# A hybrid decoder layer on one core: twelve of the 32 steps of the MLP's second product in seven products for nine, the end of the residual put first, seven weight buffers for eight

## The chip, the core and the metric

The kernel runs on one core of a Trainium2 chip. The metric is the device time of one execution in microseconds (us), lower is better. TensorE (PE) multiplies, VectorE (DVE) and ScalarE (ACT) work element by element, GpSimd (POOL) helps them, and SyncE (SP) issues the transfers from memory. Each engine runs its own list of instructions in a fixed order and stops at an instruction until what it waits for is there; everything behind that instruction waits with it.

## What is computed

One decoder layer for 256 tokens of width 2048 in float32: a norm, one input projection, a state-space group and an attention group side by side, an output projection with a residual, then a second norm and an MLP. The change touches the end of the output projection and the MLP:

```
x = x + concatenate([y_ssd, y_att], axis=-1) @ w_out
u = rmsnorm(x, g_mlp) @ w_up            # 2048 -> 8192
return x + square(relu(u)) @ w_down     # 8192 -> 2048
```

## The kernel before

**Three products for one.** A float32 operand is split into a rounded part "hi" and a rest "lo", and a product is made of hi·hi, lo·hi and hi·lo (`three`, L198, L200, L201). For each tile of weights SP loads `raw` (L150, 512 KB), ACT rounds it into the first half of a buffer `w2` (L153), and DVE subtracts to get the second half (L154). There are five `w2` buffers, and before the MLP four `raw` buffers (tag "raw"); from the MLP on four more (tag "rawm") in a pool that takes over memory of the pool `mid`, so the loads into it wait for the last users of `mid`. Weights are prepared in the order in which PE wants them, and a buffer is taken again when its last reader is done.

**Output projection and residual.** `w_out` is done in four quarters of 512 columns. After each, `residual(j)` adds the result to `xr` on DVE (L789), PE transposes it (L703), ACT scales it by the gain and rounds it (L706), and DVE makes the rest (L707); that is `x2x`, the left operand of the MLP's first product. ACT then squares the rows (L796) for the second norm. The norm's row factor is not applied to `x2x`; as `rs4` it is applied when a result is added to `xr` (L901). After the fourth quarter DVE sums the squares and makes `rs4` with 17 small instructions (L815, `rsqrt`, L817).

**The MLP in three passes.** The 32 steps of 256 hidden units are done in passes of 10, 11 and 11 (`PARTS`). In a pass `up` makes all of its steps (first product, L239, then relu and square, split into `uh` and `ul`), and `down` multiplies them with `w_down`, first for output columns 0 to 1023 (j = 0, "first half"), then for the rest ("second half"). A plain step is 8 products of 128x128x512, so 24 matmuls. For the steps of a pass whose number g is in `SEVEN` a Strassen-Winograd scheme does with 7 products, so 21 matmuls. For it `combine` makes three sums of weight blocks `t` with four POOL instructions (L861 to L864), which read and overwrite the two `raw` tiles of the step, and `combined` rounds them on ACT (L879) and takes the rest on DVE (L880) into `wt`. **There is one `t` and one `wt`.** So the wt of one such step can be rounded only after PE has done the step before it of that kind, and POOL can begin the next t only when DVE has finished this wt. In `up`, DVE makes four sums more for such a step (L838).

**The turn.** Products p1, p5, p6, p7 are summed over the steps of a half in four accumulators. After the last step of that kind, which is g = 8, DVE adds them up and empties them (L901, L934 to L940). The second half's ordinary accumulators are the same four, so PE can't begin the second half before that. Between lie g = 9 in the first pass, g = 9 and 10 in the others. The end of the first half and the start of the second is called the turn below.

**Order.** PE's instructions stand in the order in which the program issues them. For all other engines a scheduler sets the order, by place in the program and by priority: weights (`operands`, `combine`, `combined`) are raised by `HP` = 600 places. SP's loads stand in that order in one queue.

Of the kernel before, what the change touches and what calls it, by code (L numbers as in the profile page):

```python
# [1 line left out]

# [1 line left out]

# [5 lines left out]
F32 = mybir.dt.float32  # L10
# [33 lines left out]


PARTS = (0, 10, 21, 32)
SEVEN = {2, 5, 8}

A11, A21, A12, A22 = range(4)
S3, S1, S2, S4 = 1, 4, 5, 6  # L50
# [34 lines left out]
def hymba_kernel(ctx: ExitStack, tc: tile.TileContext, xn, xt, w_in, w_out, w_up, w_down, vcol, vrow, out):  # L85
# [46 lines left out]
    def raw_tile(parts, pitch):  # L132

        taken[0] += 1
        pool, tag = (mlp_pool[0], "rawm") if mlp_pool and taken[0] % 2 else (wts, "raw")
        return pool.tile([P, parts, pitch], F32, name="raw", tag=tag, bufs=RB)

    def operands(src, n, load=None, shift=0, parts=2):

# [554 lines left out]
            yield 3  # L694


    def split_rows(rows, hi, lo, k0, gain):

        for k in range(0, 4, 2):
            pt = mp("ps_sr").rearrange("p (k t) -> p k t", k=2)  # L700
            for i in range(2):
                for b in range(NB):
                    nc.tensor.transpose(pt[:, i, b * P:(b + 1) * P], rows[b][:, (k + i) * P:(k + i + 1) * P], ident)  # L703
            for i in range(2):
                kt = k0 + k + i
                nc.scalar.activation(hi[:, kt, :], pt[:, i, :], AF.Copy, scale=gain(kt))  # L706
                nc.vector.scalar_tensor_tensor(lo[:, kt, :], pt[:, i, :], gain(kt), hi[:, kt, :].bitcast(F32),  # L707
                                               op0=OP.mult, op1=OP.subtract)
            yield 0

    ys = {}

# [26 lines left out]
    def run():  # L739
        acc = in_block("k", load_x)  # L740
        spawn(head_norm(acc, [kT[:, :, b * P:(b + 1) * P] for b in range(NB)], vcp("g_k"), "k"), "k")
        acc = in_block("m0", load_n)
        spawn(stats(), "stats")
        for b in range(NB):
            evac(sm[b], acc[b][:, :96], b)
            evac(v[:, b, :208], acc[b][:, 96:M0W], b)
        spawn(index_keys(), "index_keys")
        spawn(rates(), "rates")
        for i in range(4):
            index_queries(in_pair("qi", i))  # L750
# [24 lines left out]

        def y_left(kt):
            if kt < 8:
                return yah[:, kt, :], yal[:, kt, :]
            need(f"gate{kt // 4 - 2}")
            hi, lo = ys[kt // 4 - 2]  # L780
            return hi[:, kt % 4, :], lo[:, kt % 4, :]

        ss2 = keep.tile([P, NB, 4], F32, name="ss2")
        box = []

        def residual(j, acc):
# [6 lines left out]
            yield from split_rows(rows, box[0][:, :, :T], box[0][:, :, T:], 4 * j, lambda kt: vcp("g_mlp", kt))
            for b in range(NB):
                junk = mid.tile([P, 512], F32, name="junk2", **u2)
                nc.scalar.activation(junk, rows[b], AF.Square, accum_out=ss2[:, b, j:j + 1])  # L796

        for j in range(4):
            spawn(residual(j, product(w_out[j], 512, y_left)), f"res{j}")
        return xr, box, ss2  # L800

    xr, box, ss2 = run()

    def x2(kt):
        if kt >= KT - 4:
# [6 lines left out]
    sst = keep.tile([P, NB], F32, name="sst")  # L812
    rs2 = keep.tile([P, NB], F32, name="rs2")
    rs4 = keep.tile([P, NB], F32, name="rs4")
    nc.vector.tensor_reduce(out=sst, in_=ss2, axis=AX.X, op=OP.add)  # L815
    rsqrt(rs2, sst, 1.0 / D, "x2")
    nc.vector.tensor_tensor(rs4, rs2, rs2, op=OP.mult)  # L817
    mid_stack.close()


# [3 lines left out]
    def up(h, tag):  # L824

        u = []
        for j in range(PARTS[h + 1] - PARTS[h]):
# [7 lines left out]
            if n == 7:  # L835
                for o, x, y, op in ((S1, A21, A22, OP.add), (S2, S1, A11, OP.subtract), (S3, A11, A21, OP.subtract),
                                    (S4, A12, S2, OP.subtract)):
                    nc.vector.tensor_tensor(full[:, o], full[:, x], full[:, y], op=op)  # L838
            shape = [P, 7 if j in SEVEN else 4, P]
            uh = mlp.tile(shape, F32R, name="uh", tag=f"uh{j}", bufs=1)  # L840
            ul = mlp.tile(shape, F32R, name="ul", tag=f"ul{j}", bufs=1)
            nc.scalar.copy(uh[:, :n], full[:, :n])
# [185 lines left out]
```

## Time and profile before

| | |
|---|---|
| runs | 1062.31, 1064.66, 1067.76 us; median 1064.66 |
| the profiled execution | 1066.81 us, its span from first to last instruction 1065.0 |
| TensorE clock granted in it | 0.998 |
| steps in seven products | g = 2, 5, 8 of each pass, in both halves: 18 of 64 |
| transfers | 207.41 MB, 195 GB/s over the span |

Times in rows are us from the start of the span. A matmul's duration in the rows is longer than its pitch, since matmuls overlap; where they follow each other without a gap, the pitch is the distance of two starts. In brackets stands how long the engine had been idle and what ended that.

### The profile page before, as it was taken

The page shows a single profiled execution, that of the slowest core. Times are in us where ns is not written, and L with a number is a line of the kernel's source. Part 1 is how long each engine was busy: PE and PEld are TensorE (multiplying, and loading weights), DVE is VectorE, ACT ScalarE, POOL GpSimd, SP SyncE. Part 2 cuts the span into 40 slices and gives each one's busy share as a digit, 9 for nine tenths or more (in the row PEclk, how much of TensorE's full clock was granted, in tenths as well). Part 3 has the DMA queues.
Part 4 walks back from the last instruction along what each step waited for, and adds up shares of the span by engine and source line. Part 5 has one row for each costly group of instructions (what it writes and reads, how often), then busy time and mean ns, then how long its engine had stood idle before and what let it go on. Part 6 is the DMA issues. An engine that isn't in the chain of part 4 may idle for free.

```text
span 1065.0 us, 15655 instructions
## 1 busy us (share of the span) xinstructions
PE 1057.3 (99%) x5962; PEld 936.6 (88%) x5962; DVE 785.3 (74%) x1066; ACT 555.8 (52%) x749; POOL 151.4 (14%) x102
## 2 busy tenths in 40 slices
PE   9999999999999989999999999999999999999998
PEld 7999999888888878888888889998888899988887
DVE  7776899677775656667787766768797676677885
ACT  7755464556765544454545445545544454445452
POOL 0020000122000000003352000025240000043430
PEclk9999999999999999999999999999999999999999
DMA  9865446553375565654756666547656565657561
GB/s 328 270 211 180 158 129 194 186 159 133 125 257 183 192 237 178 198 189 159 235 189 235 198 199 198 198 152 230 212 198 235 190 196 189 207 169 237 193 222 40
DMA packets 63611, 207.41 MB, mean 195 GB/s; under 512 B 7088, under 2 KB 11440, under 8 KB 63536
## 3 DMA queue, kind: packets, MB, share of 16 engines
q1 hardware_dynamic: 63392, 206.36, 58.7%
q8 instruction: 47, 0.77, 0.3%
q14 instruction: 28, 0.23, 0.1%
q10 hardware_dynamic: 144, 0.05, 0.0%
HBM read 204.29 MB, written 2.10 MB: 194 GB/s over the span
## 4 chain that ended last, share of the span: by engine, by line
PE 98%; DMA 1%; ACT 0%; DVE 0%; SPq 0%; issue 0%; ACTq 0%
PE acc L239 32%; PE acc L198 17%; PE acc L200 17%; PE acc L201 17%; PE acc L218 10%; PE ps_y L619 1%; DMA raw<-in_w_up 1%; PE ps_l L657 0%; PE ps_o L682 0%; PE ps_sr L703 0%; DMA xT<-in_xt 0%; PE ps_s L510 0%; PE ps_s L509 0%; PE ps_dec L610 0%; PE ps_pt L674 0%; DVE w L154 0%
## 5 line engine op out<-in xcount | busy, mean ns | idle before, releaser
L154 DVE TENSOR_TENSOR w<-raw,w 128x1024 fp32r<-128x1024 f32 (+3 forms) x364 | 439.4, 1218 | 197.0 <-ACT w L153 195.2
L153 ACT CAST w<-raw 128x1024 fp32r<-128x1024 f32 (+3 forms) x364 | 359.6, 993 | 330.4 <-PE acc L201 139.3
L239 PE MATMUL acc<-x2x,w 128*128 128x512 f32 (+2 forms) x2053 | 347.6, 330 | 2.7 <-DVE x2x L707 2.7
L239 PEld LDWEIGHTS acc<-x2x,w 128*128 128x128 f32 x2053 | 309.9, 188 | 39.7 <-DVE x2x L707 3.5
L198 PE MATMUL acc<-w,uh 128*128 128x512 f32 (+5 forms) x459 | 168.6, 373 | 0.0
L200 PE MATMUL acc<-w,ul 128*128 128x512 f32 (+1 forms) x444 | 168.1, 379 | 0.0
L201 PE MATMUL acc<-w,uh 128*128 128x512 f32 (+1 forms) x444 | 168.1, 379 | 0.0
L861 POOL TENSOR_TENSOR t<-raw 128x512 f32<-128x512 f32 x18 | 25.9, 1440 | 645.4 <-DMA raw<-in_w_down 482.7
L218 PE MATMUL acc<-hx,w 128*128 128x256 f32 (+1 forms) x978 | 115.0, 277 | 0.0
L218 PEld LDWEIGHTS acc<-hx,w 128*128 128x128 f32 x978 | 112.7, 188 | 0.0
L198 PEld LDWEIGHTS acc<-w,uh 128*128 128x128 f32 x459 | 85.9, 188 | 14.6
L200 PEld LDWEIGHTS acc<-w,ul 128*128 128x128 f32 x444 | 83.4, 188 | 13.7
L201 PEld LDWEIGHTS acc<-w,uh 128*128 128x128 f32 x444 | 83.3, 188 | 13.6
L198 PE MATMUL acc<-w,hx 128*128 128x512 f32 (+3 forms) x228 | 84.0, 371 | 0.3 <-ACT hx L277 0.3
L200 PE MATMUL acc<-w,hx 128*128 128x512 f32 (+1 forms) x224 | 81.0, 361 | 0.0
L201 PE MATMUL acc<-w,hx 128*128 128x512 f32 (+1 forms) x224 | 80.8, 361 | 0.0
L880 DVE TENSOR_TENSOR w<-raw,w 128x1024 fp32r<-128x1024 f32 x36 | 56.4, 1566 | 20.5 <-ACT w L879 18.4
L879 ACT CAST w<-raw 128x1024 fp32r<-128x1024 f32 x36 | 37.7, 1046 | 41.9 <-PE acc L201 36.8
L880 DVE TENSOR_TENSOR wt<-t,wt 128x1536 fp32r<-128x1536 f32 x18 | 31.6, 1757 | 25.9 <-ACT wt L879 25.9
L198 PEld LDWEIGHTS acc<-w,hx 128*128 128x128 f32 x228 | 42.8, 188 | 6.7 <-issue 0.7
L200 PEld LDWEIGHTS acc<-w,hx 128*128 128x128 f32 x224 | 42.2, 188 | 6.0 <-issue 0.7
L201 PEld LDWEIGHTS acc<-w,hx 128*128 128x128 f32 x224 | 42.1, 188 | 6.0 <-DVE w L154 0.4
(229 smaller groups left out, 1043.8 us busy)
## 6 DMA issues: line engine op xcount, KB each, us to landing
raw<-in_w_up SPq DMA_DIRECT2D x128, 512.0 KB, 4.3
raw<-in_w_down SPq DMA_DIRECT2D x128, 512.0 KB, 4.3
raw<-in_w_in SPq DMA_DIRECT2D x72, 512.0 KB, 3.9
raw<-in_w_out SPq DMA_DIRECT2D x32, 512.0 KB, 3.3
raw<-in_w_in SPq DMA_DIRECT2D x16, 256.0 KB, 5.4
raw<-in_w_in SPq DMA_DIRECT2D x16, 152.0 KB, 5.1
raw<-in_w_in SPq DMA_DIRECT2D x8, 304.0 KB, 3.2
xT<-in_xt SPq DMA_DIRECT2D x8, 256.0 KB, 5.4
```

What stands on the lines that cost most here:

```text
L153: nc.scalar.copy(hi[:, s], raw[:, s, :n])
L154: nc.vector.tensor_tensor(lo[:, s], raw[:, s, :n], hi[:, s].bitcast(F32), op=OP.subtract)
L198: nc.tensor.matmul(go(out[:, i:j]), ah, go(wh[:, i:j]), start=first and i == 0, stop=False, skip_group_check=True)
L200: nc.tensor.matmul(go(out), al, go(wh), start=False, stop=False, skip_group_check=True)
L201: nc.tensor.matmul(go(out), ah, go(wl), start=False, stop=last, skip_group_check=True)
L218: nc.tensor.matmul(acc[:, c, at:at + n], w[:, 0, s], x[:, fr:fr + n], start=(i + k + j == 0), stop=(i >= 2 and k == 7 and j == len(todo) - ...
L239: nc.tensor.matmul(walk(out[:, at:at + n]), w[:, 0, s], walk(x[:, at:at + n]), start=(i < 2 and k + j == 0), stop=(i >= 2 and k == 7 and j ...
L619: nc.tensor.matmul(pt[:, 64 * i:64 * i + 64], m[i // 4][:, i % 4, :], xdt[:, c, 64 * h:64 * h + 64], start=True, stop=True)
L861: nc.gpsimd.tensor_tensor(t[:, 0], raws[1][:, 1], raws[1][:, 0], op=OP.subtract)
L879: nc.scalar.copy(hi, raw)
L880: nc.vector.tensor_tensor(lo, raw, hi.bitcast(F32), op=OP.subtract)
```

## The change

1. `SEVEN` is {2, 4, 6, 8} instead of {2, 5, 8}: 24 of 64 half-steps in seven products. POOL's, ACT's and DVE's work for `t`, `wt` and the four sums is done for six more.
2. From the MLP on there are seven `raw` buffers, four of tag "raw" and three of tag "rawm", taken in turn, instead of eight.
3. The fourth quarter's additions, rounding and rests have a priority above that of weights (`urgent`), and its two groups of transposes stand together.
4. Its squares and the row factors are taken in the first `up`, at step 3 (`row_factors`), and write to tiles of the MLP's pool, not of `mid`.

```
-SEVEN = {2, 5, 8}
+SEVEN = {2, 4, 6, 8}
...
-        pool, tag = (mlp_pool[0], "rawm") if mlp_pool and taken[0] % 2 else (wts, "raw")
-        return pool.tile([P, parts, pitch], F32, name="raw", tag=tag, bufs=RB)
+        pool, tag, n = (mlp_pool[0], "rawm", 3) if mlp_pool and taken[0] % 7 in (1, 3, 5) else (wts, "raw", RB)
+        return pool.tile([P, parts, pitch], F32, name="raw", tag=tag, bufs=n)
...
+            with urgent():
+                for i in range(2):
+                    kt = k0 + k + i
+                    nc.scalar.activation(hi[:, kt, :], pt[:, i, :], AF.Copy, scale=gain(kt))
...
+            if urgent is nullcontext or k == 2:
+                yield 0
...
+            urgent = (lambda: tc.high_priority(offset=3 * HP)) if j == 3 else nullcontext
+            with urgent():
+                for b in range(NB):
+                    nc.vector.tensor_tensor(rows[b], rows[b], acc[b], op=OP.add)
+        def squares(j, rows, junk):
+            for b in range(NB):
+                nc.scalar.activation(junk[b], rows[b], AF.Square, accum_out=ss2[:, b, j:j + 1])
...
+    def row_factors(junk):
+
+        squares(3, [xr[:, b, 1536:] for b in range(NB)], junk)
+        nc.vector.tensor_reduce(out=sst, in_=ss2, axis=AX.X, op=OP.add)
+        rsqrt(rs2, sst, 1.0 / D, "x2")
+        nc.vector.tensor_tensor(rs4, rs2, rs2, op=OP.mult)
...
+            if h == 0 and j == 3:
+                row_factors([mlp.tile([P, 7, P], F32, name="r")[:, :4].rearrange("p k t -> p (k t)") for _ in range(NB)])
```

Lines move by 16 in the MLP: L879 and L880 become L895 and L896, L901 becomes L917, L934 to L939 become L950 to L955, and L706, L707 become L707, L708.

**ACT at the end of the output projection.** `ps_sr` are the transposes of the fourth quarter, `w2` the weights that follow, `junk2` the squares. Before:

```order
L796 ACTIVATE junk2_4065,ss2_3350<-xr_3345 128x512
L796 ACTIVATE junk2_4067,ss2_3350<-xr_3345 128x512
L706 ACTIVATE x2x_3547<-ps_sr_4024,vc_86 128x256 x2
L153 CAST w2_4151<-raw_4150 128x1024
L153 CAST w2_4172<-raw_4171 128x1024
L153 CAST w2_4193<-raw_4192 128x1024
L706 ACTIVATE x2x_3547<-ps_sr_4047,vc_86 128x256 x2
```

And now:

```order
L707 ACTIVATE x2x_3547<-ps_sr_4024,vc_86 128x256
L707 ACTIVATE x2x_3547<-ps_sr_4033,vc_86 128x256
L707 ACTIVATE x2x_3547<-ps_sr_4024,vc_86 128x256
L153 CAST w2_4148<-raw_4147 128x1024
L707 ACTIVATE x2x_3547<-ps_sr_4033,vc_86 128x256
```

The squares are gone from here, and one cast of weights stands ahead of the last of the four roundings, where three stood ahead of the last two.

**SP in the second pass, ahead of the turn.** The first two rows are weights of the second half's g = 0, the next two (L859, now L875) are those of its g = 2, which POOL combines. The brackets name whose count each load waits for. Before:

```order
L150 DMA raw_7274<-in_w_down 128x1024 [waits DMAHW6_49,DMAHW4_49,DVE_49]
L150 DMA raw_7279<-in_w_down 128x1024 [waits DMAHW7_49,DMAHW5_49,DVE_49]
L859 DMA raw_7308<-in_w_down 128x1024 [waits DVE_49,Pool_49]
L859 DMA raw_7310<-in_w_down 128x1024 [waits DVE_49]
L150 DMA raw_7317<-in_w_down 128x1024 [waits DMAHW0_49,DVE_49]
```

And now:

```order
L150 DMA raw_7296<-in_w_down 128x1024 [waits DMAHW7_49,DMAHW4_49,DVE_49]
L150 DMA raw_7301<-in_w_down 128x1024 [waits DMAHW5_49,DVE_49,Pool_49]
L875 DMA raw_7330<-in_w_down 128x1024 [waits DVE_49]
L875 DMA raw_7332<-in_w_down 128x1024 [waits DMAHW2_49,DVE_49]
L150 DMA raw_7339<-in_w_down 128x1024 [waits DMAHW0_49,DVE_49]
```

The wait for POOL has moved up by one load; what `raw_7301` takes over is the first `raw` tile of g = 8, which POOL reads last in its fourth instruction. In the first pass the same wait stood at the load behind the two of g = 2 and now stands at the second of the two.

**DVE in the second pass, at the turn.** `wt_7357` and now `wt_7379` belong to the second half's g = 2; `r` are sums of the accumulators; `w2_7280`, `w2_7323` and now `w2_7302`, `w2_7345` are weights of the second half's g = 0 and g = 1. Before:

```order
L934 TENSOR_TENSOR r_7187<-r_7187,acc_6949 128x512
L935 TENSOR_TENSOR r_7188<-r_7187,acc_6950 128x512
L880 TENSOR_TENSOR wt_7357<-t_7312,wt_7357 128x1536
L901 SCALAR_TENSOR_TENSOR xr_3345<-r_7188,rs4_4113,xr_3345 128x512
L937 TENSOR_TENSOR r_7187<-r_7187,acc_6948 128x512
L939 TENSOR_TENSOR r_7188<-r_7188,acc_6948 128x512
L154 TENSOR_TENSOR w2_7280<-raw_7279,w2_7280 128x1024
```

And now:

```order
L950 TENSOR_TENSOR r_7209<-r_7209,acc_6966 128x512
L951 TENSOR_TENSOR r_7210<-r_7209,acc_6967 128x512
L896 TENSOR_TENSOR wt_7379<-t_7334,wt_7379 128x1536
L917 SCALAR_TENSOR_TENSOR xr_3345<-r_7210,rs4_4108,xr_3345 128x512
L953 TENSOR_TENSOR r_7209<-r_7209,acc_6965 128x512
L955 TENSOR_TENSOR r_7210<-r_7210,acc_6965 128x512
L154 TENSOR_TENSOR w2_7302<-raw_7301,w2_7302 128x1024
```

Nothing moved here: as before, the next half's wt stands between the first and the last of the sums, ahead of weights that PE needs sooner. In the first pass it stands in the same place.

## Rows read from the trace of the kernel before

**Rows 1.** The page's first part: busy us, share of the span, instructions.

```profile
PE 1057.3 (99%) x5962; PEld 936.6 (88%) x5962; DVE 785.3 (74%) x1066; ACT 555.8 (52%) x749; POOL 151.4 (14%) x102
```

**Rows 2.** Who waited for whom, of PE: us in total, times, longest.

```profile
PE acc L239 <- DVE x2x L707: 2.7, 2, 2.4
```

**Rows 3.** The timeline of all engines from the last matmuls of the output projection into the MLP's first product.

```profile
384.52 0.63 ACT L796 ACTIVATE junk<-xr 128x512 f32<-128x512 f32 x1 [1.89 <-DVE xr L789]
...
390.01 2.00 ACT L153 CAST w<-raw 128x1024 fp32r<-128x1024 f32 x2 [0.49 <-DMA raw<-in_w_up]
...
392.54 1.04 ACT L153 CAST w<-raw 128x1024 fp32r<-128x1024 f32 x1 [0.52 <-DMA raw<-in_w_up]
393.49 0.47 ACT L706 ACTIVATE x2x<-ps_sr,vc 128x256 fp32r<-128x256 f32 x1
...
395.27 0.47 ACT L706 ACTIVATE x2x<-ps_sr,vc 128x256 fp32r<-128x256 f32 x1 [1.31 <-DVE x2x L707]
395.29 0.30 PEld L239 LDWEIGHTS acc<-x2x,w 128*128 128x128 f32 x2 [2.74 <-DVE x2x L707]
395.29 0.79 PE L239 MATMUL acc<-x2x,w 128*128 128x512 f32 x2 [2.44 <-DVE x2x L707]
...
396.31 3.80 PEld L239 LDWEIGHTS acc<-x2x,w 128*128 128x128 f32 x15 [0.73 <-DVE x2x L707]
```

**Rows 4.** The timeline of PE in the second product: in the first pass the first matmul of g = 8 of the first half, of g = 9, and the first matmul of the second half that writes p5's accumulator; in the second pass the first matmul of g = 8, and the matmuls that first read the lo of `w2_7280` and of `w2_7323`.

```profile
540.53 0.38 PE L198 MATMUL acc<-w,uh 128*128 128x512 f32 x1
...
545.15 0.38 PE L198 MATMUL acc<-w,uh 128*128 128x512 f32 x1
...
551.75 0.38 PE L198 MATMUL acc<-w,uh 128*128 128x512 f32 x1
...
759.94 0.38 PE L198 MATMUL acc<-w,uh 128*128 128x512 f32 x1
...
776.88 0.38 PE L201 MATMUL acc<-w,uh 128*128 128x512 f32 x1
...
782.16 0.38 PE L201 MATMUL acc<-w,uh 128*128 128x512 f32 x1
```

**Rows 5.** Groups of instructions by line and shape: count, busy us, mean ns of one, idle time before them.

```profile
L880 DVE TENSOR_TENSOR wt<-t,wt 128x1536 fp32r<-128x1536 f32 x18 | 31.6, 1757 | 25.9 <-ACT wt L879 25.9
...
L838 DVE TENSOR_TENSOR r<-r 128x128 f32<-128x128 f32 x36 | 11.8, 349 | 0.6
...
L879 ACT CAST wt<-t 128x1536 fp32r<-128x1536 f32 x18 | 26.5, 1474 | 39.8 <-POOL t L864 27.0 <-PE acc L201 12.8
```

**Rows 6.** Line L880's instructions on the two `raw` tiles: shortest, median and longest duration in ns.

```profile
L880 DVE TENSOR_TENSOR w<-raw,w x36: 1208/1226/2309, 503.1 to 1040.7; 128x1024 fp32r<-128x1024 f32 x36
```

**Rows 7.** The timeline of POOL: the start of the combination for the second half's g = 2 in the first pass; then the first and the last instruction of that combination in the second pass; then of one in its second half.

```profile
534.76 1.29 POOL L861 TENSOR_TENSOR t<-raw 128x512 f32<-128x512 f32 x1 [8.77 <-DMA raw<-in_w_down]
...
759.51 1.28 POOL L861 TENSOR_TENSOR t<-raw 128x512 f32<-128x512 f32 x1 [14.61 <-DMA raw<-in_w_down]
...
765.35 2.15 POOL L864 TENSOR_TENSOR t<-raw,t 128x512 f32<-128x512 f32 x1
...
793.89 1.28 POOL L861 TENSOR_TENSOR t<-raw 128x512 f32<-128x512 f32 x1 [7.86 <-DVE wt L880]
...
798.85 2.15 POOL L864 TENSOR_TENSOR t<-raw,t 128x512 f32<-128x512 f32 x1
```

**Rows 8.** The timeline of DVE in the first pass: the wt of g = 5, then, at the turn, the wt of the second half's g = 2 and the first and the last of the sums behind it.

```profile
516.55 1.76 DVE L880 TENSOR_TENSOR wt<-t,wt 128x1536 fp32r<-128x1536 f32 x1 [0.15 <-ACT wt L879]
...
548.12 1.75 DVE L880 TENSOR_TENSOR wt<-t,wt 128x1536 fp32r<-128x1536 f32 x1
549.78 0.74 DVE L901 SCALAR_TENSOR_TENSOR xr<-r,rs,xr 128x512 f32<-128x512 f32 x1
...
551.04 0.68 DVE L939 TENSOR_TENSOR r<-r,acc 128x512 f32<-128x512 f32 x1
```

**Rows 9.** The timeline of ACT: the wt of g = 5 in the first pass, and the wt of the second half's g = 2 in the second pass.

```profile
515.04 1.48 ACT L879 CAST wt<-t 128x1536 fp32r<-128x1536 f32 x1 [0.99 <-PE acc L201]
...
767.53 1.47 ACT L879 CAST wt<-t 128x1536 fp32r<-128x1536 f32 x1 [3.71 <-POOL t L864]
```

**Rows 10.** The timeline of DVE at the turn of the second pass: the wt of the second half's g = 2, then `w2_7280` and `w2_7318`, then `w2_7323`.

```profile
769.82 1.75 DVE L880 TENSOR_TENSOR wt<-t,wt 128x1536 fp32r<-128x1536 f32 x1
...
773.34 2.35 DVE L154 TENSOR_TENSOR w<-raw,w 128x1024 fp32r<-128x1024 f32 x2
...
778.91 1.50 DVE L154 TENSOR_TENSOR w<-raw,w 128x1024 fp32r<-128x1024 f32 x1
```

**Rows 11.** The timeline of SP: the two loads for the combination that begins at 534.76.

```profile
528.25 1.47 SPq L859 DMA_DIRECT2D raw<-in_w_down  x2
```

**Rows 12.** The page's sixth part: issues, KB each, median us from issue to landing.

```profile
raw<-in_w_down SPq DMA_DIRECT2D x128, 512.0 KB, 4.3
```

**Rows 13.** Busy us of each engine and instructions in two stretches, with clock, DMA share and GB/s: one in the first `up`, one in the first half of the first pass.

```profile
432.00:443.00 11.00, 11.00 (x66) 9.73 (x65) 6.86 (x8) 5.30 (x9) 0.00 (x0) 1.00 0.64 195
500.00:530.00 30.00, 30.00 (x141) 25.71 (x140) 25.50 (x21) 17.22 (x19) 13.88 (x8) 1.00 0.67 225
```

More of the change, by code (lines that the diff above doesn't have):

```diff
@@ L1 @@
-from contextlib import ExitStack
+from contextlib import ExitStack, nullcontext
 import numpy as np
@@ L694, in attention, with split_rows @@
             yield 3
-    def split_rows(rows, hi, lo, k0, gain):
+    def split_rows(rows, hi, lo, k0, gain, urgent=nullcontext):
         for k in range(0, 4, 2):
@@ L703, in split_rows @@
                     nc.tensor.transpose(pt[:, i, b * P:(b + 1) * P], rows[b][:, (k + i) * P:(k + i + 1) * P], ident)
[L704 to L709, printed above, removed]
+            with urgent():
+                for i in range(2):
+                    kt = k0 + k + i
+                    nc.scalar.activation(hi[:, kt, :], pt[:, i, :], AF.Copy, scale=gain(kt))
+                    nc.vector.scalar_tensor_tensor(lo[:, kt, :], pt[:, i, :], gain(kt), hi[:, kt, :].bitcast(F32),
+                                                   op0=OP.mult, op1=OP.subtract)
+            if urgent is nullcontext or k == 2:
+                yield 0
     ys = {}
@@ L784, in run @@
         box = []
+        def squares(j, rows, junk):
+            for b in range(NB):
+                nc.scalar.activation(junk[b], rows[b], AF.Square, accum_out=ss2[:, b, j:j + 1])
         def residual(j, acc):
             rows = [xr[:, b, 512 * j:512 * j + 512] for b in range(NB)]
-            for b in range(NB):
-                nc.vector.tensor_tensor(rows[b], rows[b], acc[b], op=OP.add)
+            urgent = (lambda: tc.high_priority(offset=3 * HP)) if j == 3 else nullcontext
+            with urgent():
+                for b in range(NB):
+                    nc.vector.tensor_tensor(rows[b], rows[b], acc[b], op=OP.add)
             yield Y["res"] if j < 3 else 1
@@ L792, in residual @@
                 box.append(keep.tile([P, KT, 2 * T], F32R, name="x2x", tag="hx"))
[L793 to L796, printed above, removed]
+            yield from split_rows(rows, box[0][:, :, :T], box[0][:, :, T:], 4 * j, lambda kt: vcp("g_mlp", kt),
+                                  urgent)
+            if j < 3:
+                squares(j, rows, [mid.tile([P, 512], F32, name="junk2", **u2) for _ in range(NB)])
         for j in range(4):
             spawn(residual(j, product(w_out[j], 512, y_left)), f"res{j}")
-        return xr, box, ss2
-    xr, box, ss2 = run()
+        return xr, box, ss2, squares
+    xr, box, ss2, squares = run()
     def x2(kt):
@@ L814, in hymba_kernel @@
     rs4 = keep.tile([P, NB], F32, name="rs4")
-    nc.vector.tensor_reduce(out=sst, in_=ss2, axis=AX.X, op=OP.add)
-    rsqrt(rs2, sst, 1.0 / D, "x2")
-    nc.vector.tensor_tensor(rs4, rs2, rs2, op=OP.mult)
+    def row_factors(junk):
[3 more added lines that the diff above has]
+        nc.vector.tensor_tensor(rs4, rs2, rs2, op=OP.mult)
     mid_stack.close()
```

## Prediction

> **What bounds the kernel now.** First the busy shares: PE is busy for 1057.3 of 1065.0 us, so only fewer matmuls, or a wait of PE that goes or comes, can move the end [rows 1]. Then PE's waits: but for the first microseconds they name one place, 2.7 us where the first product of the MLP needs `x2x` [rows 2]. Then the timeline there: three casts of later weights stand ahead of the last two roundings, and the third waits for a load; ACT rounds at 393.49 and 395.27 what PE wanted 2.44 us before 395.29 [rows 3]. Last the second product, where PE never waits; the question is by how much the others are ahead of it. DVE is busy for 25.50 of 30 us there [rows 13], and the turn shows the margin: the last sum that empties p5's accumulator ends at 551.04 + 0.68 = 551.72, and PE's first matmul into it starts at 551.75 [rows 4, 8]. **There is no slack at the turn of the first pass.**
>
> **Fewer matmuls.** 21 of them take 545.15 - 540.53 = 4.62 us, so 0.220 each, and a plain step of 24 takes 5.28 [rows 4]. Three steps more in two halves save three matmuls each: 18 x 0.220 = **4.0 us**, all on the path.
>
> **The end of the residual.** PE's idle time of 2.44 us and the small one behind it make the 2.7 us [rows 2, 3]. Three of the four roundings now stand ahead of any cast, with the transposes together. The last stands behind one cast, whose load no longer waits for the squares, that is until 384.52 and over a microsecond of ACT. If the load starts with the end of the output projection, at about 384.2, and takes the median 4.3 us [rows 12] or, several together, some two more, then a cast, a rounding and a rest (1.04 + 0.47 + 0.5) make it ready by 390.5 to 392.5; PE wants it just past 395.29 - 2.44 = 392.85. So the stall goes: **2.7 us**. Ends: 0.5 less where the load is late, and 3.5 by the weight loads' idle times (2.74 + 0.73) [rows 3].
>
> **Costs that I put at nothing.** The 17 small instructions and two squares move into an `up` where DVE is idle for 4 of 11 us and ACT for more than 5 [rows 13], with five `w2` buffers between them and PE; uncovered they would cost some 3 us once. The four sums for one step more per pass (4 x 0.35 us [rows 5]) lie in the same slack. Seven loads under way for eight matter nothing in `up`, where a tile lasts PE longer than the 4.3 us that it takes to land.
>
> **The loop of t and wt.** This is the cost that decides. With steps of that kind two apart, PE has 21 + 24 = 45 matmuls, 9.9 us, for one round of the loop. The round: POOL's four instructions, 759.51 to 767.50, so 8.0 us, or 793.89 to 801.00, so 7.1 [rows 7]; ACT's wt 1.47; DVE's wt 1.76 [rows 5]; three handovers of 0.03 to 0.08. That is **10.5 to 11.4 us**: longer than PE's 9.9. (Three apart, PE needed 15.2, and the loop had time to wait.) I take 8.0 for POOL: its long instructions of 2.15 us fall beside DVE's, and DVE has more to do now.
>
> Let S be the start of g = 8 in the first half. PE ends g = 2 114 matmuls before it, at S - 25.1. ACT starts the wt of the next such step 0.25 us after that (515.04, where by the matmuls g = 2 ends at 540.53 - 117 x 0.22 = 514.79), and DVE ends it at 518.31 [rows 8, 9]: S - 21.6. Two rounds later the wt of g = 8 is ready, at S - 0.6 to S + 1.2. PE wants it at S + 2.6, after four products, so it is in time by 1.4 us at worst. But the loop arrives late at the turn, and there the next half's wt stands in DVE's list ahead of what PE needs.
>
> **First pass.** POOL is through with g = 8 3.3 us before its wt, at S - 3.9 to S - 2.1. With seven buffers the second load for the next combination waits for that; it lands 4.3 us later (3.3 to 5.4; the two loads issued from 528.25 on were waited for until 534.76 [rows 7, 11, 12]). POOL runs from then, or from when t is free, takes 7.1 to 8.0, and rounding and rest take 3.3: wt at S + 9.9 to S + 14.6. Before: 549.87 - 540.53 = S + 9.3 [rows 4, 8]. At POOL's 8.0 and 4.3 for the load it is S + 13.5, 4.2 later. The next combination then starts beside the sums, and the first of these (0.67 us in its place) reads two operands from SBUF as L880 does, which goes from 1226 to 2309 ns beside POOL [rows 6]: 0.6 more. With no margin, PE waits **4.8 us** (0.6 to 5.9).
>
> **Second and third pass, each.** One plain step more lies in between, but now the wait for POOL stands one load ahead of both loads for the combination, so three are issued at POOL's end. At 225 GB/s with a share of 0.67 [rows 13] 512 KB take 1.6 us at full rate: the last lands after 4.4 to 7.5, and I take 6.0. POOL starts at S + 3.9 and wt is there at S + 15.2 (10.9 to 16.7), against 771.57 - 759.94 = S + 11.6 before: 3.6 later. Two weights behind it run beside POOL, 1.1 us longer each [rows 6], and one that was slowed by 0.3 is no longer. `w2_7323` had ended at 780.4 for a matmul at 782.16 [rows 4, 10], a margin of 1.75: 3.6 + 2.2 - 0.3 - 1.75 = **3.75 us** (0 to 5.5). The wait comes in two pieces, at g = 0 and g = 1 of the second half. Second halves have no turn of this kind behind them: nothing.
>
> Sum: + 4.8 + 2 x 3.75 - 4.0 - 2.7 = **+ 5.6 us** on the span of 1065.0, so 1070.6; the runs' median stands 0.3 below this span (and the profiled execution 1.8 above), so **1070.3**. Ends of the terms: + 0.6 - 4.0 - 3.5 = - 6.9, and 5.9 + 11.0 - 4.0 - 2.2 = + 10.7.
>
> What POOL and DVE do to each other is shown by rows: 1.28 for 2.15 us and 1226 for 2309 ns [rows 6, 7]. The Trainium skill, page "SBUF — State Buffer", section "Who interferes with whom", says that a DVE instruction with two SBUF inputs contends with a reading GpSimd, and that the loser fully blocks for the whole instruction. The long POOL instruction agrees only roughly: 2.15 us is less than 1.28 + 1.21. Taken strictly it gives the fourth rival.
>
> **Rivals.**
> 1. *The cover holds*, the one that ends faster. Price: nothing at the turns, - 6.7, so 1058. It decides at POOL's 7.1 us: then the loop slips only 0.6 a round, and quick loads leave the turn where it was. For it: PE never waited here before. Against: the margin of 0.03 us, and that ACT already waited 3.71 us for POOL at the second turn with steps three apart [rows 9].
> 2. *Only the first turn stalls*: the extra plain step hides the others. 4.8 - 6.7: 1063.
> 3. *The residual keeps its stall* because the load ahead of the last rounding is late as before: 2.7 more than forecast, 1073. Against: what it waited for has gone.
> 4. *POOL blocks for a whole DVE instruction*: 1.28 + 1.21 = 2.5 for 2.15, a combination of 10.2 for 8.0 us; three in a row up to the turn are 6.6 more in three passes: 20 us, 1090. For it: 2309 ns is near 1226 + 1280. Against: 2.15 was the longest usual row.
>
> **How the numbers follow.** About 0.5% is what a measurement of this kernel can tell from no change: below 1059.3 is faster, above 1070.0 slower. The forecast, stalls of 9 to 17 us in all, has 58%, of which 36 above 1070.0 and 22 below. Rival 1 has 13% (12 faster, 1 the same), rival 2 15% (the same), rival 3 6% and rival 4 8% (slower). Faster 12%, the same 22 + 1 + 15 = 38%, slower 36 + 6 + 8 = 50%. The range 1060 to 1077 leaves out most of rival 1 and of rival 4. The sign is less sure than the mechanism: the forecast lies on the edge of what can be told.
>
> **What would show it.** Right: PE's matmuls fall by 18 x 128x512; no wait for `x2x`; PE waits at the first turn for L955, by 3 to 6 us, and at the other two for L154 by 2 to 6 each, in two pieces; ACT's wait for POOL grows from 27.0 us, and POOL's rounds in a half are over 10.5 us apart. Wrong: no wait of PE at the turns (rival 1), waits at wt itself (rival 4), or a wait for `x2x` still there (rival 3).

## The result: slower, by twice the forecast

The changed kernel takes 1075.80 us (median of 1073.67, 1075.61, 1075.99 and 1077.47), the kernel before 1064.83 in the same runs: ratio 1.0104, 95% interval 1.0083 to 1.0124, so **+11.0 us** where + 5.6 was forecast. The profiled execution took 1073.67, with a span of 1071.9 against 1065.0.

**Where PE waits.** The view of waits, PE alone: us in total, times, longest.

```profile
PE acc L201 <- DVE w L154: 6.9, 4, 3.1
PE acc L198 <- DVE r L955: 3.8, 1, 3.8
```

The wait for `x2x` [rows 2] is gone; instead PE waits once for p5's accumulator (the first turn) and in two pieces each at the other two turns (the four times of L154): 10.7 us in all, where 12.3 was forecast. So waits grew by 8.0 and 4.0 us of matmuls went, which would make + 4.0. The rest is not in this view.

**The turns.** The timelines of ACT, DVE and POOL. ACT's rows are the wt of g = 6, of g = 8 and of the second half's g = 2 in the first pass, then the wt of the second half's g = 2 in the second pass. DVE's rows are the same two wt of a second half and what stands behind them; POOL's row is the start of the combination for the second of them.

```profile
519.93 1.47 ACT L895 CAST wt<-t 128x1536 fp32r<-128x1536 f32 x1 [2.47 <-POOL t L880]
...
531.34 1.48 ACT L895 CAST wt<-t 128x1536 fp32r<-128x1536 f32 x1 [1.61 <-POOL t L880]
...
543.61 1.47 ACT L895 CAST wt<-t 128x1536 fp32r<-128x1536 f32 x1 [6.09 <-POOL t L880]
...
768.27 1.47 ACT L895 CAST wt<-t 128x1536 fp32r<-128x1536 f32 x1 [7.46 <-POOL t L880]
```

```profile
545.11 1.76 DVE L896 TENSOR_TENSOR wt<-t,wt 128x1536 fp32r<-128x1536 f32 x1 [1.38 <-ACT wt L895]
...
548.05 0.68 DVE L955 TENSOR_TENSOR r<-r,acc 128x512 f32<-128x512 f32 x1
...
769.77 1.76 DVE L896 TENSOR_TENSOR wt<-t,wt 128x1536 fp32r<-128x1536 f32 x1 [5.46 <-ACT wt L895]
...
773.30 3.44 DVE L154 TENSOR_TENSOR w<-raw,w 128x1024 fp32r<-128x1024 f32 x2
```

```profile
761.96 2.19 POOL L877 TENSOR_TENSOR t<-raw 128x512 f32<-128x512 f32 x1 [7.47 <-DVE w L154]
```

The round of the loop is 531.34 - 519.93 = 11.4 us, then 12.3 across the turn. ACT waits for POOL, DVE for ACT, and PE for what stands behind the wt in DVE's list: 548.05 + 0.68 = 548.73, and PE starts at 548.79. Before, DVE came to the same wt without waiting [rows 8, 10].

The matmul that waits is the tenth of the second half: the first starts at 542.80, and the first row here is the ninth. The second row is the tenth in the kernel before:

```profile
544.56 0.39 PE L201 MATMUL acc<-w,uh 128*128 128x512 f32 x1
```

```profile
552.41 0.38 PE L198 MATMUL acc<-w,uh 128*128 128x512 f32 x1
```

The last sum had ended at 551.72 [rows 8], so the kernel before had a margin of 0.69 us here.

**What a wait left behind.** PE's timeline in the first pass, behind its wait of 3.84 us, and 48 us later; then in the second pass, behind the longest wait.

```profile
548.79 0.50 PE L198 MATMUL acc<-w,uh 128*128 128x512 f32 x1 [3.84 <-DVE r L955]
549.12 0.39 PE L200 MATMUL acc<-w,ul 128*128 128x512 f32 x1
...
596.62 0.39 PE L201 MATMUL acc<-w,uh 128*128 128x512 f32 x1
596.85 0.39 PE L198 MATMUL acc<-w,uh 128*128 128x512 f32 x1
597.08 0.38 PE L200 MATMUL acc<-w,ul 128*128 128x512 f32 x1
597.30 0.39 PE L201 MATMUL acc<-w,uh 128*128 128x512 f32 x1
...
783.30 0.79 PE L201 MATMUL acc<-w,uh 128*128 128x512 f32 x1 [3.09 <-DVE w L154]
783.89 0.63 PE L198 MATMUL acc<-w,uh 128*128 128x512 f32 x1
784.32 0.63 PE L200 MATMUL acc<-w,ul 128*128 128x512 f32 x1
...
789.36 0.38 PE L200 MATMUL acc<-w,ul 128*128 128x512 f32 x1
789.58 0.38 PE L201 MATMUL acc<-w,uh 128*128 128x512 f32 x1
```

Stretches around that last wait: length, busy PE, matmuls in brackets, granted clock, DMA share and GB/s:

```profile
775.00:780.00 5.00, 5.00 (x24) 1.00 0.61 210
780.00:785.00 5.00, 1.91 (x5) 0.74 0.13 35
785.00:790.00 5.00, 5.00 (x14) 0.57 0.98 304
790.00:795.00 5.00, 5.00 (x24) 1.00 0.83 272
```

Two things follow a wait. **The clock:** behind the wait at 783 the clock is at its lower level, 1.2 GHz (0.43 between starts for 0.22, until 789.0): thirteen matmuls in 5.7 us for 2.9. **The pitch:** in the first pass the clock is 1.00, and yet starts are 0.23, 0.23, 0.22 apart instead of 0.220 [rows 4], and stay so to the end of the half: 597.30 - 549.12 is 48.18, or 211 matmuls at 0.2283, 1.8 us more than at 0.220. No idle time is shown, and PE counts as busy. The first product has it too. PE busy in L239 alone, the first `up` of the kernel before, then that of the changed one (columns as above):

```profile
380.00:500.00 120.00, 112.37 (x643) 0.99 0.59 194
```

```profile
380.00:500.00 120.00, 107.37 (x642) 1.00 0.62 202
```

The same matmuls took 5.0 us more behind the wait for `x2x`, beside its 2.7 us of idle time; the clock is part of it, as a view of the kernel before shows (0.66 for 5 us, 1.7 us lost):

```profile
395.00:400.00 5.00, 4.47 (x16) 0.66 0.65 214
```

Stage by stage, from the starts of the stages' first matmuls in the two timelines:

| stage | before | after | difference |
|---|---|---|---|
| up to the first `up` | 384.02 | 384.49 | + 0.5 |
| first `up` | 115.28 | 107.84 | - 7.4 |
| first `down` | 101.95 | 106.58 | + 4.6 |
| second `up` | 117.46 | 117.44 | 0.0 |
| second `down` | 112.51 | 119.03 | + 6.5 |
| third `up` | 117.45 | 117.45 | 0.0 |
| third `down`, to the last matmul | 112.86 | 115.56 | + 2.7 |

That is the + 6.9 of the two spans. The + 0.5 lies ahead of the MLP; that stretch takes 382.9 to 385.2 us in the runs below. The profiled execution of the changed kernel was the quickest of its four (granted clock 0.997; the others 0.995, 0.994 and 0.994), and that of the kernel before was one of its slower ones.

### The profile page after: what moved, and what is told of

Same layout as the page of the kernel before. It is cut to its first block, busy times and chain, and to the rows that moved or that the text cites. A ratio compares the mean times of both kernels' runs of the same rounds, so it can differ in the third digit from the quotient of the medians.

```text
span 1071.9 us, 15705 instructions
## 1 busy us (share of the span) xinstructions
PE 1055.4 (98%) x5943; PEld 932.2 (87%) x5943; DVE 818.1 (76%) x1084; ACT 562.3 (52%) x755; POOL 201.7 (19%) x126
## 4 chain that ended last, share of the span: by engine, by line
PE 75%; POOL 9%; issue 6%; DVE 4%; DMA 4%; ACT 1%; SPq 0%; POOLq 0%; DVEq 0%
PE acc L239 26%; PE acc L201 12%; PE acc L198 11%; PE acc L200 11%; PE acc L218 10%; DMA raw<-in_w_down 4%; POOL raw L878 3%; DVE w L154 2%; POOL t L879 2%; POOL t L877 2%; POOL t L880 2%; DVE xr L917 1%; ACT wt L895 1%; PE ps_y L619 1%; DMA xT<-in_xt 1%
## 5 line engine op out<-in xcount | busy, mean ns | idle before, releaser
L154 DVE TENSOR_TENSOR w<-raw,w 128x1024 fp32r<-128x1024 f32 (+3 forms) x352 | 428.2, 1225 | 175.0 <-ACT w L153 174.6
L153 ACT CAST w<-raw 128x1024 fp32r<-128x1024 f32 (+3 forms) x352 | 346.2, 991 | 302.3 <-PE acc L201 115.7
L239 PE MATMUL acc<-x2x,w 128*128 128x256 f32 (+2 forms) x2052 | 342.6, 327 | 0.0
L239 PEld LDWEIGHTS acc<-x2x,w 128*128 128x128 f32 x2052 | 307.9, 188 | 34.2
L198 PE MATMUL acc<-w,uh 128*128 128x512 f32 (+4 forms) x435 | 161.5, 377 | 3.8 <-DVE r L955 3.8
L877 POOL TENSOR_TENSOR t<-raw 128x512 f32<-128x512 f32 x24 | 39.3, 1636 | 613.7 <-DMA raw<-in_w_down 277.0
L896 DVE TENSOR_TENSOR w<-raw,w 128x1024 fp32r<-128x1024 f32 x48 | 87.4, 1833 | 6.0 <-ACT w L895 5.5
L895 ACT CAST w<-raw 128x1024 fp32r<-128x1024 f32 x48 | 50.3, 1048 | 37.6 <-PE acc L201 19.1
L895 ACT CAST wt<-t 128x1536 fp32r<-128x1536 f32 x24 | 35.4, 1474 | 65.3 <-POOL t L880 62.8
L896 DVE TENSOR_TENSOR wt<-t,wt 128x1536 fp32r<-128x1536 f32 x24 | 42.2, 1757 | 33.4 <-ACT wt L895 33.1
L198 PEld LDWEIGHTS acc<-w,hx 128*128 128x128 f32 x228 | 42.7, 188 | 7.5 <-ACT w L153 1.1
L878 POOL TENSOR_TENSOR raw<-raw 128x512 f32<-128x512 f32 x24 | 47.5, 1977 | 1.9
```

Of the source, the lines that this page charges most:

```text
L153: nc.scalar.copy(hi[:, s], raw[:, s, :n])
L154: nc.vector.tensor_tensor(lo[:, s], raw[:, s, :n], hi[:, s].bitcast(F32), op=OP.subtract)
L198: nc.tensor.matmul(go(out[:, i:j]), ah, go(wh[:, i:j]), start=first and i == 0, stop=False, skip_group_check=True)
L239: nc.tensor.matmul(walk(out[:, at:at + n]), w[:, 0, s], walk(x[:, at:at + n]), start=(i < 2 and k + j == 0), stop=(i >= 2 and k == 7 and j ...
L877: nc.gpsimd.tensor_tensor(t[:, 0], raws[1][:, 1], raws[1][:, 0], op=OP.subtract)
L878: nc.gpsimd.tensor_tensor(raws[1][:, 0], raws[1][:, 0], raws[0][:, 0], op=OP.subtract)
```

## The experiments

Theory A: a wait of PE costs its length and, behind it, a lower clock for some us and a wider pitch. B: a wait costs its length alone. C: the seven buffers make the turns wait. D: the loop of t and wt is too slow at distance two, whatever stands where at the turn. Each table line gives the medians of the kernel and of the kernel before on the same chip.

| run | us | before | difference | ratio, 95% interval |
|---|---|---|---|---|
| e1_three | 1061.22 | 1063.63 | - 2.4 | 0.9970 to 0.9986 |
| e1b_three_eight | 1059.77 | 1063.63 | - 3.9 | 0.9956 to 0.9980 |
| e2_seven_only | 1076.62 | 1063.63 | + 13.0 | 1.0109 to 1.0154 |
| e3_hold | 1061.28 | 1063.63 | - 2.4 | 0.9970 to 1.0003 |
| e4_wait | 1067.75 | 1063.98 | + 3.8 | 1.0014 to 1.0044 |
| e5_wait_cuts | 1064.06 | 1063.98 | + 0.1 | 0.9996 to 1.0015 |
| e6_short_wait | 1059.57 | 1063.98 | - 4.4 | 0.9948 to 0.9975 |
| e7_best | 1058.08 | 1063.98 | - 5.9 | 0.9935 to 0.9969 |
| e8_twenty_two | 1059.61 | 1064.01 | - 4.4 | 0.9947 to 0.9974 |
| e9_after_cuts | 1075.25 | 1064.01 | + 11.2 | 1.0081 to 1.0126 |
| e10_urgent | 1060.06 | 1064.01 | - 4.0 | 0.9951 to 0.9975 |
| e11_wait_again | 1068.21 | 1064.01 | + 4.2 | 1.0025 to 1.0057 |
| e13_hold_first_22 | 1058.23 | 1064.14 | - 5.9 | 0.9931 to 0.9960 |
| e14_pool_three | 1056.44 | 1064.14 | - 7.7 | 0.9912 to 0.9938 |
| e15_after_again | 1076.23 | 1064.14 | + 12.1 | 1.0080 to 1.0145 |

**The parts of the change.** e1_three is the changed kernel with

```
-SEVEN = {2, 4, 6, 8}
+SEVEN = {2, 5, 8}
```

> The changed kernel with SEVEN back at {2, 5, 8}: the new residual, the late row factors and seven raw buffers alone. A (a wait of PE costs its length, and behind it a lower granted clock for some us and a wider pitch of matmuls to the end of the stage): no wait for x2x, no low clock behind it, first up 107.8 us as in the changed kernel and not 115.3; 1064.8 - 7.4 = 1057.4, and no wait at a turn. B (a wait costs its length and no more): 1064.8 - 2.7 = 1062.1. C (seven buffers are what makes the turns wait): waits of 1 to 3 us at the turns here too, 1060 to 1066.

e1b_three_eight has the eight buffers of before as well:

> The same with eight raw buffers as before: the residual and the late row factors alone. A: 1057.4, within 1 us of the run with seven. B: 1062.1. C: 3 to 6 us less than with seven.

e2_seven_only is the kernel before with `SEVEN = {2, 4, 6, 8}` and the seven buffers:

> The kernel before with SEVEN {2, 4, 6, 8} and seven raw buffers, its residual as it was: four seven-product steps a half alone. A: the wait for x2x and its 7.4 us stay, so 1075.8 + 7.4 = 1083. B: 1075.8 + 2.7 = 1078.5. In both PE waits at the turns for 3 to 4 us each, in the first pass for L939 and in the others for L154.

e10_urgent is the kernel before with the `urgent` lines alone:

> The kernel before with the priority of the residual's last quarter alone: squares and row factors stay where they were, SEVEN {2, 5, 8}, eight buffers. All four roundings now stand ahead of the casts of the first weights, and the squares ahead of both. If the order on ACT was what made PE wait for x2x: the wait goes, 1059.8 as with the late row factors. If the late load was it (it waits for the squares): PE waits 1 to 3 us for the first weights of up instead, 1061 to 1064.

e10 and e1b give the same - 4.0 and - 3.9: the priority alone is enough, and the late squares and row factors add nothing that can be measured. PE waits nowhere in the MLP in either, and their first `up` is busy for 107.37 as in the changed kernel. The median gain lies between B (2.7) and A's 7.4; A's figure came from a dear execution. Of the 23 executions of the kernel before beside e1b those with a clock of 0.998 took 1062.8 to 1066.7 and those with 1.0 took 1061.8 to 1063.3; beside e10, on another chip, some with 1.0 took up to 1066.6, so the clock is not all of it.

Seven buffers for eight cost 1.4 us in the medians (e1 against e1b), but the two intervals overlap. In the profiles the difference is 1.3 us, all of it in the second half of the first pass, where e1's starts are 0.2233 apart and e1b's 0.220; an execution with eight buffers shows the same pitch there (e5, below). So C is not shown. With {2, 4, 6, 8} eight buffers were not run; e3 and e13 below keep the seven and lose the waits for L154.

e2 carries the whole loss, with waits of 2.9 and 7.1 us at the same lines as the changed kernel (its L939 is L955 there). A's 1083 was missed (B's 1078.5 lies inside the interval), and what both took for granted doesn't hold: its profile has no wait for `x2x` either. ACT there, in the numbers of the kernel before:

```profile
390.73 1.05 ACT L153 CAST w<-raw 128x1024 fp32r<-128x1024 f32 x1
391.69 0.47 ACT L706 ACTIVATE x2x<-ps_sr,vc 128x256 fp32r<-128x256 f32 x1
```

One cast stands ahead of the last rounding, as in the changed kernel, and PE is busy in its first `up` for 107.77. So e2's own edits, the buffers or the four steps, change the order on ACT without the priority, and beside them the priority adds nothing that can be measured (1076.62 against 1075.80). If its other executions lack that wait too, the turns cost e2 13.0 + 4.0 for the matmuls + 4.0 for the residual = 21 us.

**The order at the turn.** e3_hold makes the second half's wt wait for the weights that PE needs sooner:

```
 w = combined(ahead, w[1][1][1][:, :1] if j == 1 and g == min(marked) else None) if seven ...
...
+    if n == 3 and hold is not None:
+        nc.vector.tensor_copy(hi[:, 0, :1], hold)
     nc.scalar.copy(hi, raw)
```

> The changed kernel, but the wt of the second half's g = 2 waits for the second half's g = 1: a copy of one column from its last w2 into wt ahead of ACT's rounding. Everything else as in the changed kernel. A: no wait at a turn, and with the waits their clock and pitch go too: 1064.8 - 7.4 - 4.0 = 1053.4. B: 1075.8 - 10.7 = 1065.1. D (the loop of t and wt itself is too slow for steps two apart, whatever its place in the order at the turn): waits for wt of 1 to 4 us in a half, 1058 to 1070.

One instruction of 0.14 us in each second half (L896, a copy of one column) takes 13.4 us off the changed kernel (+ 11.0 to - 2.4). PE's waits:

```profile
PE acc L201 <- DVE wt L898: 2.1, 2, 1.1
...
PE acc L198 <- DVE r L957: 0.9, 1, 0.9
```

Waits fell by 7.7 us and the time by 13.4: B is refuted. The 1053.4 was missed, though, and D explains part: in the first pass, where the sums still came 0.9 late, wt is twice late by 1.07. ACT's wt there:

```profile
565.12 1.48 ACT L897 CAST wt<-t 128x1536 fp32r<-128x1536 f32 x1 [1.60 <-POOL t L880]
...
576.51 1.47 ACT L897 CAST wt<-t 128x1536 fp32r<-128x1536 f32 x1 [1.60 <-POOL t L880]
...
587.92 1.47 ACT L897 CAST wt<-t 128x1536 fp32r<-128x1536 f32 x1 [1.61 <-POOL t L880]
```

Rounds of 11.4 us, and PE takes 9.9 for one. e14_pool_three leaves out one of POOL's four instructions in it, L878's `raws[1][:, 0] - raws[0][:, 0]`, so that it computes no layer:

> As e3_hold (1061.3, two waits of 1.07 us for wt in the first pass, rounds of 11.4 us), with POOL's second instruction of four left out, which takes the difference of two blocks in place; the products of the steps concerned are then not the layer's. D: rounds of 9.3 to 10 us, no wait for wt, 1056 to 1059. If POOL's share of the round isn't what sets it (DVE's and ACT's order is): rounds stay near 11, waits for wt stay.

```profile
562.62 1.47 ACT L896 CAST wt<-t 128x1536 fp32r<-128x1536 f32 x1 [4.80 <-POOL t L879]
...
572.65 1.48 ACT L896 CAST wt<-t 128x1536 fp32r<-128x1536 f32 x1 [3.64 <-POOL t L879]
...
582.69 1.48 ACT L896 CAST wt<-t 128x1536 fp32r<-128x1536 f32 x1 [4.78 <-POOL t L879]
```

Rounds of 10.0, no wait for wt, 1056.4: POOL's share sets the round, and the loop is D's, but it is worth some 5 us at the most, not the 20 or so of the turns.

e14 also gives a price by stage, since its profile has the changed kernel's 5943 matmuls and no wait in the MLP. By the starts of the stages its three `down` are 1.32 us shorter each than e1b's: the 4.0 us of the 18 matmuls. Those of the changed kernel are 5.9, 7.8 and 4.0 us longer than e14's, **17.8 us for 10.7 of waiting**; e2's are 19.9 longer for 10.3.

**The price of a wait by itself.** e4_wait puts a wait into e1b, where there was none; e6_short_wait has the same with `(3, 0)` and `range(2)`:

```
+if h > 0 and j == 1 and g == 1:
+    spare = [mlp.tile([P, 7, P], F32, name="r").rearrange(...) for _ in range(2)]
+    with tc.high_priority(offset=3 * HP):
+        for i in range(4):
+            nc.scalar.copy(spare[i // 2][:, 448 * (i % 2):448 * (i % 2) + 448], outs[(3, 2, 1, 0)[i]][:, :448])
```

> The kernel with the new residual, SEVEN {2, 5, 8} and eight buffers (1059.8), in which PE waited nowhere in the MLP, with one wait put in at the start of g = 1 of the second half, in the second and third pass: ACT copies 448 columns of each of the four open accumulators to unused memory, and PE's next matmul into the last of them waits for that. Two waits of 2.5 to 3.3 us. A (a wait of PE costs its length, and behind it a lower granted clock for some us and a wider pitch of matmuls to the end of the half): 2 x 3 for the waits, 0 to 3.4 each for the clock, 0.8 to 1.8 each for the pitch of the 220 matmuls behind: 1068 to 1074, clock 0.995 to 0.998. B (a wait costs its length): 1066, clock 1.0.

> The same without splits, with two copies instead of four: two waits of 1.2 to 2.2 us. A: the pitch widens as behind the longer wait, the clock falls more rarely: 2 x 1.7 + 2 x 1.3 + 0 to 2 = 1065 to 1068. B: 1063.

> The same kernel as e4_wait, for a second profile: e4_wait's profiled execution was its fastest (1061.9, pitch 0.220 throughout), its median 1067.8 at a clock of 1.0. If the wider pitch is what the slower ones pay, a profile of a usual one shows two waits of 1.5 us as before, clock 1.0, and a pitch of 0.223 to 0.229 from one or both waits to the end of the half, or a longer third up.

In e6 no wait came about, against the expectation: both copies ran under matmuls that don't need them, and its 1059.57 is e1b's 1059.77. So the two copies cost nothing, and e4's two waits of 1.54 us (shorter than expected) cost 1067.75 - 1059.57 = **8.2 us for 3.1 of waiting, at a clock of 0.999 to 1.0**: neither B nor the clock, but the pitch. The first profile was of an execution without it, the second, e11, with. PE behind the first of the two waits, in e4 and then in e11:

```profile
773.56 0.49 PE L198 MATMUL acc<-w,uh 128*128 128x512 f32 x1 [1.54 <-ACT r L964]
773.89 0.39 PE L200 MATMUL acc<-w,ul 128*128 128x512 f32 x1
774.12 0.38 PE L201 MATMUL acc<-w,uh 128*128 128x512 f32 x1
774.34 0.38 PE L198 MATMUL acc<-w,uh 128*128 128x512 f32 x1
...
822.30 0.38 PE L201 MATMUL acc<-w,uh 128*128 128x512 f32 x1
```

```profile
775.49 0.50 PE L198 MATMUL acc<-w,uh 128*128 128x512 f32 x1 [1.54 <-ACT r L964]
...
777.17 0.38 PE L200 MATMUL acc<-w,ul 128*128 128x512 f32 x1
...
825.86 0.38 PE L198 MATMUL acc<-w,uh 128*128 128x512 f32 x1
```

The wait is the same to the hundredth. In e4 the 219 matmuls from 774.12 to 822.30 are 0.220 apart; in e11 the 218 from 777.17 to 825.86 are 0.2233 apart. And e11's third `up`, which begins behind such a half, is busy for 120.73 us where e4's takes 117.61 (L239, the first row e4, the second e11):

```profile
820.00:960.00 140.00, 117.61 (x705) 1.00 0.61 194
```

```profile
820.00:960.00 140.00, 120.73 (x705) 1.00 0.58 188
```

So the wider pitch takes 0.7 us in each half, and something like it outlives the stage: 3.1 us in the `up` between them. In all, from the first `up` on, e4's profile is 3.7 us longer than e1b's, and e11's 8.3, for the same 3.1 us of waits.

e5_wait_cuts adds to e4 split matmuls behind the waits, such as `CUTS` makes where a first half begins:

```
+if h > 0 and j == 1:
+    cut = {8 + at: n for at, n in CUTS.items()}
```

> The same with five matmuls of the steps behind the wait split in two, as the kernel does it at the start of each first half (CUTS). A: the waits as in the run without splits, the pitch back at 0.220 within 6 us of the wait, so 1 to 3 us less; the clock falls as there. If the pitch has nothing to do with the wait, no change or up to 1 us more for the splits.

It took 3.7 us off e4, with the same two waits of 1.54 in its profile, where the pitch is 0.220 again from 785 on; but e4's own profile is back at 0.220 without splits, so only the medians speak for them.

The profile of e5 is of its slowest execution, 1066.83, and shows something else. In its first pass, where it has none of the copies and added splits and so is e1b, no matmul waits, and yet the starts of the second half are 0.2233 apart, and the second `up` behind it is busy for 120.73 us (L239):

```profile
590.00:716.00 126.00, 120.73 (x705) 1.00 0.58 186
```

What does wait is the weight load ahead of the tenth matmul of that half, for the last sum. PE's weight loads in e5, then in e1_three, whose second half has the same pitch:

```profile
544.02 0.19 PEld L198 LDWEIGHTS acc<-w,uh 128*128 128x128 f32 x1 [0.17 <-DVE r L957]
```

```profile
544.17 0.19 PEld L198 LDWEIGHTS acc<-w,uh 128*128 128x128 f32 x1 [0.18 <-DVE r L955]
```

In the profiles of the kernel before, e1b, e4, e6, e10 and e11 the sum ends 0.6 to 0.9 us ahead of that matmul, no weight load waits there, and the pitch stays at 0.220. So a fifth of a us at the wrong place was followed by 0.8 us of pitch and 3.1 in the next `up`.

e9_after_cuts has such splits in the second halves of the changed kernel:

> The changed kernel with five split matmuls also in the second halves: from the start in the first pass, from the step behind the second wait in the others. The waits at the turns stay, 10 to 11 us in all, and the clock still falls behind some. A (the wider pitch is a cost of its own): pitch 0.220 within some 6 us of the waits, so 1 to 5 us less than the changed kernel's 1075.8: 1071 to 1075. B (a wait costs its length alone): 1075.8 or a little more for the splits.

It gained nothing (+ 11.2 for + 11.0). In its profile the second pass is back at 0.220 and the first is not, and PE's waits at the turns are 12.9 us for 10.7. Splits help sometimes; what decides it was not found.

e15_after_again is the changed kernel again:

> The changed kernel once more, for a second profile beside the first and more executions on the same chip as the two others: waits at the same three places, 3 to 4 us each; what lies behind them differs between executions: clock 0.994 to 0.997, pitch of 0.220 to 0.229 to the end of the half, and an up of 117.4 or of some 120.5 us behind a half of wider pitch. Sum: 1055.8 + 10.7 for the waits + 3 to 7 for the clock + 3 to 6 for the pitch: 1073 to 1079.

Its two executions took 1072.39 (clock 0.997) and 1080.08 (0.994). The slower was profiled: waits of 11.0 us, the lower clock behind three of them, the pitch wide in all three second halves, and its third `up` at 120.73. From the first `up` on it is 24.8 us longer than e14.

**Kernels without the waits.** e8_twenty_two leaves out step 8 in the first pass, where one plain step less lies at the turn; e13_hold_first_22 holds wt behind the first weight of g = 1 instead of the second:

```
-n = 7 if j in SEVEN else 4
+n = 7 if j in SEVEN and (h, j) != (0, 8) else 4
-marked = SEVEN
+marked = SEVEN if h else SEVEN - {8}
...
-combined(ahead, w[1][1][1][:, :1] if j == 1 ...
+combined(ahead, w[1][0][1][:, :1] if j == 1 ...
```

> As e3_hold, and in the first pass only steps 2, 4 and 6 in seven products, in both halves: 22 half-steps of 64, with 12 fewer matmuls than the kernel before. Theory A: no wait at a turn: the residual's gain as in the run with eight buffers (3.9), and 12 x 0.22 = 2.6: 1063.8 - 3.9 - 2.6 = 1057.3; up to 1.4 more with seven buffers. D: waits for wt in the second and third pass, 1060 or more.

> As e8_twenty_two (1059.6, with one wait of 1.1 us for wt at the fourth step of that kind of a half, and wider pitch in two halves), but wt of the second half's g = 2 is held behind the first weight of g = 1 and not the second, so the loop of t and wt starts its rounds 1 to 2.5 us earlier behind the turn. D (the loop's round of 11.4 us against PE's 9.9 is what is left): no wait for wt, no wider pitch: 1057.3. Otherwise (the second weight of g = 1 is now late behind wt): waits for L154 of up to 1.5 us, 1060 to 1063.

> The changed kernel with the wt of the second half's g = 2 held behind the weights of g = 1, as in e3_hold, and in the first half of the first pass, where e3_hold still waited for the sums and then twice for wt, with steps 2, 4 and 6 in seven products (23 half-steps of 64 and not 24). Theory A: no wait of PE in the MLP, clock 1.0: 1059.8 - 4.0 + 0.7 = 1056.5, faster than both kernels; with the 1.4 us that seven buffers cost beside eight, 1057.9. D (the loop of t and wt is too slow at distance two in any place): waits for wt of 1 us each in several halves, 1060 or more.

e8 missed by 2.3 us: a wait of 1.08 for wt in the second pass, and a wider pitch around it. e13 has no wait in the MLP in its profile, all three `up` at the short length, and 1058.23: **faster than both kernels**, 5.9 us under the one before and 17 to 18 under the changed one. The profile is of one of its quicker executions: three took 1056.2 to 1057.2 and three 1059.2 to 1059.9, and what the second three pay was not profiled. In e7 the first half of the first pass multiplies a sum where step 8 needs a block, so it is no layer; by its time, 1058.08, 23 half-steps can't be told from the 22 of e13 and e8, nor the place of the hold in e13 from that in e8: the intervals of all three overlap.

## Why the forecast had the right sign and half the size

- **Fewer matmuls, - 4.0:** right; 18 matmuls at 0.220, seen in e14 as 3 x 1.32.
- **The residual, - 2.7:** the mechanism was right (the order on ACT, shown by e10, and by e2, where that order came about without the priority) and rival 3 falls. The size was not: - 4.0 in medians, - 7.4 in the profiled pair. I took the wait's idle time for its price.
- **Costs put at nothing:** the late squares and row factors cost nothing (e10 and e1b). For the seven buffers a reason was wrong: in `up` a tile of 512 KB lasts PE 2.7 us (at 195 GB/s [rows 13]), not longer than the 4.3 that it takes to land. The second `up` takes 117.44 us with seven and 117.46 with eight all the same.
- **The loop:** forecast 10.5 to 11.4 us a round; 11.4, and 12.3 across the turn. Rivals 1 and 2 fall: all three turns waited.
- **The turns' waits, 4.8 and twice 3.75:** measured 3.84, 3.64 and 3.26, at the lines and in the pieces that were named. 12.3 was 10.7. The first was too long because "no slack" was a misreading: the matmul at 551.75 is not the one that waits for the sum, the tenth of the half at 552.41 is. With that margin of 0.69 the 4.8 would have been 4.1. (The upper end of the others is 5.25 by its own terms, not 5.5.)
- **The step that failed** is the one that was not written as a step: "4.8 + 2 x 3.75 - 4.0 - 2.7" adds waits to the span as if a us of waiting were a us of time. With the measured waits and the measured residual the same sum is 10.7 - 4.0 - 4.0 = + 2.7, and + 11.0 came; that the forecast lay nearer is luck, since its two wrong sizes both pushed it up. The turns cost 11.0 + 4.0 + 4.0 = 19 us in the medians for 10.7 of waiting, and 17.8 in the first profile. There the 7.1 beyond the waits are 2.8 of clock (the thirteen matmuls behind 783) and 4.2 of pitch (2.10, 1.36 and 0.76 in the three second halves); slower executions pay more of both (clocks of 0.994 to 0.997 over 1074 us are some 3.2 to 6.4 us, an estimate; 3.1 more where an `up` follows suit). A warning was there: the kernel before had a granted clock of 0.998, and 0.66 behind its wait for `x2x`, to which I gave no meaning. Why the pitch widens stays open.
- **Rival 4** falls as a sum: a combination took mostly 8.0 us (6.3 and 6.9 ahead of the second and third turn), not 10.2. What it rests on exists, below.

## What to carry to other kernels

Where an engine is busy for 99% of the span, a wait of it is not priced by its length: look at how long the same instructions take behind it, by pitch and by clock, until the stage ends; here 1.5 to 2.7 us for each us of waiting, by the medians. A loop through one buffer that is slower than its consumer does harm first where its output stands ahead of more urgent work in another engine's list, so hold it back there: one copy of a single column in each second half was worth more than all that the change saved. And profile a kernel that varies twice: of two executions with the same 3.1 us of waits, one paid 5.2 us behind them and one 0.6.

## What the chip showed that I had not expected

**PE has more than one steady pitch at the same granted clock.** 128x512 matmuls ran at 0.220, 0.2233 or 0.2283 us in long stretches without a gap, and left 0.220 at a wait. A short one was enough: 0.17 and 0.18 us of the weight load alone in e5 and e1_three, 0.30 us of PE in the first half of e2's first pass (0.2283 behind it). Not every wait does it: two of 1.54 in e4 and those of 0.88 and 1.07 (the first of the two) in e3_hold left 0.220. An `up` behind a half of wider pitch took 120.57 us for 117.45 in e5, e11 and e15, and not in the changed kernel's first profile or in e2. What sets the pitch is open.

**The lower clock comes with longer waits, not always.** Two waits of 1.54 us left it at 0.999 to 1.0 in all of e4's executions; those in the changed kernel cost it in every one, but in the first profile at only one of three turns (behind 3.09 us, and not behind 3.84 or 2.99). In e15 it fell behind 2.46, and in the kernel before behind 2.44.

**One POOL instruction can stand still through several of DVE's.** The same 128x512 instruction that takes 1.28 us alone took 5.60 in e3_hold, on POOL:

```profile
554.54 5.60 POOL L877 TENSOR_TENSOR t<-raw 128x512 f32<-128x512 f32 x1 [10.18 <-DVE wt L898]
```

and on DVE, at the same time:

```profile
554.38 1.22 DVE L898 TENSOR_TENSOR w<-raw,w 128x1024 fp32r<-128x1024 f32 x1
555.51 2.35 DVE L154 TENSOR_TENSOR w<-raw,w 128x1024 fp32r<-128x1024 f32 x2
557.79 1.22 DVE L898 TENSOR_TENSOR w<-raw,w 128x1024 fp32r<-128x1024 f32 x1
```

DVE's four, with two inputs in SBUF each, end at 559.01, all at their short length; POOL ends 1.13 us later, at 560.14. The Trainium skill, page "SBUF — State Buffer", section "Who interferes with whom", says that whoever issues first keeps the shared ports for the whole instruction and the other fully blocks. This row agrees: DVE was first, and its four instructions without a pause held POOL as one would.
